# Memory attention in ten small steps, the compressed branch in nine, and groups begun one unit earlier

## The chip, the cores and the metric

The kernel runs on one core of one Trainium2 chip. The metric is the time of one execution in device microseconds (us); of several runs the median counts. Engines are named as in the profile: PE (TensorE), DVE (VectorE), ACT (ScalarE), POOL (GpSimd), SP (the queue that issues the weight loads).

## What is computed

A transformer block with three mixers and a feed-forward part, followed by two layers of a second kind, on a sequence of 512 tokens of 1024 features, all in fp32. Three pieces matter here. The memory attention has four heads over 256 memory tokens:

```python
s = jnp.einsum('bshd,bmhd->bhsm', qh, k).astype(jnp.float32) * MEM_SCALE
p = jax.nn.softmax(s, axis=-1).astype(v.dtype)
return jnp.einsum('bhsm,bmhd->bshd', p, v).reshape(B, S, MEM_W)
```

The sparse attention has 16 heads in four groups, and three branches with a sigmoid gate each; the compressed branch attends to 31 averaged blocks of keys:

```python
s = jnp.einsum('bsghd,bngd->bghsn', q, kc) * NSA_SCALE
p = masked_softmax(s, end[None, :] <= t[:, None])
o = jnp.einsum('bghsn,bngd->bsghd', p.astype(vc.dtype), vc)
...
y_nsa = (gb[..., 0:1] * o_cmp + gb[..., 1:2] * o_slc + gb[..., 2:3] * o_win).reshape(B, S, NSA_Q)
```

The three mixers are then merged, `y` being the sum that the last projection completes:

```python
y = (gm[:, :, 0] * (y_nsa @ w_proj_nsa[l]) + gm[:, :, 1] * (y_ml @ w_proj_ml[l])
     + gm[:, :, 2] * (y_mem @ w_proj_mem[l]))
```

## The kernel before

All weights stream through SBUF in units of four or eight blocks of 128 x 128. To keep fp32 precision every operand is split into a high half (a cast to fp32r on ACT) and a low half (the difference, on DVE): for weights `whi` (L96) and `wlo` (L97), for activations the helper `split` (L241, L242). One product is then three matmuls (high-high, low-high, high-low, helper `mm` at L224), and one block of a unit is a step of three matmuls. SP loads a unit five units ahead, ACT and DVE split it three units ahead, between the other work of their queues.

The order of work is that in which the program issues instructions; each engine runs its own part of it in order. `mix_items` (L1619) writes the list of units. A `Mix` lays a generator between the steps of its units: it gets so many pulls, spread evenly over the steps, and with `drain` the generator is run to its end there. `Side` lets a generator go on beside the units that follow. `em.defer(n, f)` issues f some n steps later.

`mem_pair` (L1279) is a generator for two memory heads: `score` issues the score matmuls (ps_ms, 128 x 512), DVE's maximum and its negation (mmx), ACT's exponentials (mp), and DVE's reciprocal and scaling; `turn` transposes on PE (ps_mt) and splits (mpth, mptl); `values` multiplies with the values (ps_mo) and splits. Pair 0 lies between the four units that give the keys and values of the compressed branch, whose results leave a bank of ps_z by two copies on DVE (cz, L1224 and L1225) and two on ACT (cmpAk, L1226 and L1227), and beside `ml_final`, a normalisation on DVE (mfy, mfr). Pair 2 lies between gate units (ACT's sg, L1537) and projections.

`nsa_group` (L1366) treats one of four groups of sparse attention in 38 pulls. Pulls 0 to 31 each begin one of 32 scores (ps_sc; 4 heads, 2 branches, 4 blocks of 128 to 512 columns); a pull also carries the earlier scores on: maximum (smx) one pull later, exponential (pf) two, reciprocal and scaling three, transposition on PE (ps_tr) four, and its split (pth on ACT, ptl on DVE, L1484) five pulls later:

```python
stages = ((score, 0), (turn, 4), (recip, 3), (rowmax, 1), (scale, 3), (evict, 5), (low, 5), (expo, 2))
```

The compressed branch is tied to some pulls by `extra`. It shares the three banks of scores (psc) and the two banks of transposes (ptr) with the rest. Before each group come its key unit, two query units (whose split moves halves by DMA, L1347 and L1348) and its values' unit, which ends in a transposition (ps_tt) and DVE's split of the values (vs). The group's pulls are spread over fill units (merge gates and projections, 48 steps), and what is left is drained in the next group's first two units; that of the last group runs beside `p1`, the last eight projections. In `proj_unit` (L1541) a projection's result is multiplied with its gate (yt) and added to y (L1556), both on DVE; the last pass then splits y.

Of the kernel before, what the change touches and what calls it, by code (L numbers as in the profile page):

```python
# [204 lines left out]
class Model:  # L205
# [1073 lines left out]
    def mem_pair(self, h0):  # L1279
# [3 lines left out]
        pr, pt_ = {}, {}  # L1283

        def score(h, hf):
            qh, ql = self.qm[h]
            ps = self.psc.tile([P, 2, 256], F32, tag="sc", name="ps_ms")
            for t in range(2):
                xs = slice((2 * hf + t) * P, (2 * hf + t + 1) * P)
                self.mm3(ps[:, t, :], qh[:, xs], ql[:, xs], self.mk_h[:, h, :], self.mk_l[:, h, :], True, True)  # L1290
            mx = t2.tile([P, 2], F32, tag="mmx", name="mmx", bufs=3)
            nc.vector.tensor_reduce(out=mx, in_=ps, axis=AX.X, op=OP.max)
            nc.vector.tensor_scalar(out=mx, in0=mx, scalar1=-sc, scalar2=None, op0=OP.mult)
            p = t2.tile([P, 2, 256], F32, tag="mp", name="mp", bufs=3)
            sm = t2.tile([P, 2], F32, tag="msm", name="msm", bufs=3)
            for t in range(2):
                nc.scalar.activation(out=p[:, t, :], in_=ps[:, t, :], func=AF.Exp, scale=sc, bias=mx[:, t:t + 1],
                                     accum_out=sm[:, t:t + 1])
            nc.vector.reciprocal(mx, sm)
# [3 lines left out]
            pr[h, hf] = p  # L1303

        def turn(h, hf):
            p = pr.pop((h, hf))
# [10 lines left out]
        def values(h):  # L1317
# [5 lines left out]
            self.split(self.bh[h], self.bl[h], po)  # L1323

        h1 = h0 + 1
        for step in (((score, h0, 0),), ((score, h0, 1),), ((score, h1, 0),), ((turn, h0, 0),),
                     ((turn, h0, 1), (score, h1, 1)), (), ((values, h0), (turn, h1, 0)), ((turn, h1, 1),), (),
                     ((values, h1),)):
            for f, *args in step:
                f(*args)  # L1330
            yield

# [33 lines left out]
    def nsa_group(self, g):  # L1366
# [7 lines left out]
        def c_score():  # L1374
            kc = self.kc[:, g].rearrange("p c n -> p (c n)")
            cs = t3.tile([P, S], F32, tag="cpf", name="cs")
            for i in range(0, 4, 2):
                pc = self.psc.tile([P, 2, 4, 64], F32, tag="sc", name="ps_c")
                for t in range(2):
                    for j in range(4):  # L1380
                        self.mm(pc[:, t, j, :], qs[j][:, (i + t) * P:(i + t + 1) * P], kc, True, True)
                c = cs.rearrange("p (i j n) -> p i j n", i=4, j=4)[:, i:i + 2]
                nc.vector.tensor_tensor(out=c, in0=pc[:, :, :, 0:32],
                                        in1=self.maskc[:, i:i + 2].unsqueeze(2).to_broadcast([P, 2, 4, 32]), op=OP.add)
                nc.vector.tensor_tensor(out=c, in0=pc[:, :, :, 32:64], in1=c, op=OP.add)
            mx = t3.tile([P, 16], F32, tag="cmx", name="cmx")
# [3 lines left out]
            cst["p"], cst["m"] = cs, mx  # L1390
# [4 lines left out]
        def c_norm():  # L1395
            ce, mx = cst["p"], cst["m"]
            sm = t3.tile([P, 16], F32, tag="csm", name="csm")
# [5 lines left out]
            nc.vector.tensor_scalar(out=sm[:, 0:4], in0=sm[:, 0:4], scalar1=self.rowv, scalar2=None, op0=OP.mult)  # L1403
            nc.vector.tensor_tensor(out=f3(ce), in0=f3(ce), in1=sm.unsqueeze(2).to_broadcast([P, 16, 32]), op=OP.mult)
# [7 lines left out]
        def c_evict():  # L1412
            self.split(pch, pcl, cst["t"])
# [3 lines left out]
        extra = {2: c_score, 3: c_exp, 4: c_norm, 7: c_turn, 8: c_evict}  # L1417
# [123 lines left out]
    def proj_unit(self, name, idx, m, hl, first, last=False):  # L1541
# [7 lines left out]
        def done(ps):  # L1549
# [69 lines left out]
    def mix_items(self):  # L1619
# [114 lines left out]
        items += qkv[0]  # L1734
# [211 lines left out]
```

## Time and profile before

| | before |
|---|---|
| median of 3 runs | 2894.15 us (2893.62 to 2895.26) |
| the profiled execution | 2895.78 us, span of its instructions 2893.8 us |
| busy: PE, DVE, ACT, POOL | 2832.3, 1593.5, 1132.5, 29.6 us |
| mean granted clock of PE | 0.989 |

The span runs from the first to the last instruction of the profiled execution, and all starts below count from its begin. Busy time of PE overlaps: matmuls are pipelined, each is listed longer than the distance to the next. PEclk is the share of full speed that was granted.

### The profile page before, as it was taken

The page shows a single profiled execution, that of the slowest core. Times are in us where ns is not written, and L with a number is a line of the kernel's source. Part 1 is how long each engine was busy: PE and PEld are TensorE (multiplying, and loading weights), DVE is VectorE, ACT ScalarE, POOL GpSimd, SP SyncE. Part 2 cuts the span into 40 slices and gives each one's busy share as a digit, 9 for nine tenths or more (in the row PEclk, how much of TensorE's full clock was granted, in tenths as well). Part 3 has the DMA queues.
Part 4 walks back from the last instruction along what each step waited for, and adds up shares of the span by engine and source line. Part 5 has one row for each costly group of instructions (what it writes and reads, how often), then busy time and mean ns, then how long its engine had stood idle before and what let it go on. Part 6 is the DMA issues. An engine that isn't in the chain of part 4 may idle for free.

```text
span 2893.8 us, 33730 instructions
## 1 busy us (share of the span) xinstructions
PE 2832.3 (98%) x13103; PEld 2317.8 (80%) x13103; DVE 1593.5 (55%) x2504; ACT 1132.5 (39%) x1993; POOL 29.6 (1%) x111
## 2 busy tenths in 40 slices
PE   8999999999999999999999999999999999999998
PEld 6778787787788888788888888888888887788887
DVE  7765577778664344643447434454344588654443
ACT  6453355555342222422335322333223466532223
POOL 0000000000000000000000000000000000000000
PEclk9999999999999999999999999999999999999999
DMA  5222321221322323323222223232232311132322
GB/s 178 73 71 88 91 66 59 66 70 34 131 91 87 107 93 97 103 89 108 93 81 88 96 87 110 80 108 96 88 109 81 102 52 37 66 110 81 109 82 78
DMA packets 83951, 255.86 MB, mean 88 GB/s; under 512 B 9648, under 2 KB 11312, under 8 KB 83792
## 3 DMA queue, kind: packets, MB, share of 16 engines
q1 hardware_dynamic: 78528, 243.03, 26.5%
q0 software_dynamic: 3968, 8.59, 1.2%
q8 instruction: 102, 1.67, 0.2%
q10 hardware_dynamic: 1296, 2.10, 0.2%
q14 instruction: 57, 0.47, 0.1%
HBM read 246.86 MB, written 2.10 MB: 86 GB/s over the span
## 4 chain that ended last, share of the span: by engine, by line
PE 90%; DVE 6%; ACT 2%; issue 1%; DMA 0%; SPq 0%; DVEq 0%; ACTq 0%
PE ps_d L224 21%; PE ps_g L224 21%; PE ps_u L224 21%; PE ps_z L224 9%; PE ps_t L224 4%; PE ps_pj L224 2%; PE ps_c L224 2%; PE ps_pv L224 2%; PE ps_b L224 2%; PE ps_a L224 2%; PE ps_o L224 2%; PE ps_sc L224 1%; PE ps_tr L1467 1%; DVE wlo L97 1%; ACT whi L96 1%
## 5 line engine op out<-in xcount | busy, mean ns | idle before, releaser
L97 DVE TENSOR_TENSOR wlo<-raw,whi 128x1024 fp32r<-128x1024 f32 (+3 forms) x519 | 561.0, 1084 | 571.0 <-ACT whi L96 568.9
L96 ACT CAST whi<-raw 128x1024 fp32r<-128x1024 f32 (+3 forms) x519 | 483.8, 936 | 585.1 <-PE ps_d L224 259.9
L224 PE MATMUL ps_g<-xh,whi 128*128 128x512 f32 x880 | 345.5, 393 | 4.6 <-ACT xh L447 4.6
L224 PE MATMUL ps_d<-hh,whi 128*128 128x512 f32 x880 | 345.9, 393 | 0.0
L224 PE MATMUL ps_d<-hh,wlo 128*128 128x512 f32 x880 | 345.0, 392 | 0.0
L224 PE MATMUL ps_g<-xl,whi 128*128 128x512 f32 x880 | 343.8, 391 | 1.0 <-DVE xl L449 1.0
L224 PE MATMUL ps_d<-hl,whi 128*128 128x512 f32 x880 | 344.7, 392 | 0.0
L224 PE MATMUL ps_u<-xh,whi 128*128 128x512 f32 x880 | 343.9, 391 | 0.0
L224 PE MATMUL ps_g<-xh,wlo 128*128 128x512 f32 x880 | 343.4, 390 | 0.0
L224 PE MATMUL ps_u<-xl,whi 128*128 128x512 f32 x880 | 342.9, 390 | 0.0
L224 PE MATMUL ps_u<-xh,wlo 128*128 128x512 f32 x880 | 342.8, 390 | 0.0
L377 DVE TENSOR_TENSOR fu<-ps_u,R 128x512 f32<-128x512 f32 x110 | 75.9, 690 | 272.5 <-PE ps_u L224 272.5
L241 ACT CAST hh<-fh 128x512 fp32r<-128x512 f32 x110 | 68.4, 621 | 360.7 <-DVE fh L379 360.7
L224 PEld LDWEIGHTS ps_g<-xh,whi 128*128 128x128 f32 x880 | 166.0, 189 | 40.4 <-ACT xh L447 5.2
L224 PEld LDWEIGHTS ps_g<-xl,whi 128*128 128x128 f32 x880 | 165.9, 189 | 36.8 <-DVE xl L449 2.0
L224 PEld LDWEIGHTS ps_d<-hh,wlo 128*128 128x128 f32 x880 | 165.0, 188 | 37.7
L224 PEld LDWEIGHTS ps_d<-hl,whi 128*128 128x128 f32 x880 | 165.2, 188 | 37.2
L224 PEld LDWEIGHTS ps_d<-hh,whi 128*128 128x128 f32 x880 | 165.1, 188 | 37.0
L224 PEld LDWEIGHTS ps_g<-xh,wlo 128*128 128x128 f32 x880 | 165.9, 189 | 34.7
L224 PEld LDWEIGHTS ps_u<-xh,whi 128*128 128x128 f32 x880 | 165.6, 188 | 35.0 <-issue 0.5
L224 PEld LDWEIGHTS ps_u<-xl,whi 128*128 128x128 f32 x880 | 165.6, 188 | 34.8 <-issue 0.5
L224 PEld LDWEIGHTS ps_u<-xh,wlo 128*128 128x128 f32 x880 | 165.6, 188 | 34.6
(471 smaller groups left out, 4393.1 us busy)
## 6 DMA issues: line engine op xcount, KB each, us to landing
raw<-in_f2in_dram SPq DMA_DIRECT2D x176, 512.0 KB, 3.3
raw<-in_wz_dram SPq DMA_DIRECT2D x64, 512.0 KB, 3.3
raw<-in_f2dn_dram SPq DMA_DIRECT2D x64, 384.0 KB, 3.1
raw<-in_f1in_dram SPq DMA_DIRECT2D x44, 512.0 KB, 3.3
raw<-in_f2dn_dram SPq DMA_DIRECT2D x64, 320.0 KB, 2.9
raw<-in_pw_dram SPq DMA_DIRECT2D x24, 512.0 KB, 3.4
raw<-in_f1dn_dram SPq DMA_DIRECT2D x16, 384.0 KB, 3.1
raw<-in_f1dn_dram SPq DMA_DIRECT2D x16, 320.0 KB, 2.9
```

The costliest lines, as they stand in the source:

```text
L96: self.nc.scalar.copy(hi[:, 0:n], r)
L97: fn = lambda: self.nc.vector.tensor_tensor(out=lo[:, 0:n], in0=r, in1=hi[:, 0:n].bitcast(F32), op=OP.subtract)
L224: self.nc.tensor.matmul(out, lhsT, rhs, start=start, stop=stop)
L241: nc.scalar.copy(hi, src)
L377: nc.vector.tensor_tensor(out=u, in0=ps, in1=self.R, op=OP.mult)
L1467: nc.tensor.transpose(ps[:, s * P:(s + 1) * P], p[:, s * P:(s + 1) * P], self.ident)
```

## The change

`mem_pair` is cut into smaller steps. Exponentials, normalisation and the low halves of the two splits become functions of their own, each issued one pull or more after what it needs. In `nsa_group` the compressed branch takes pulls 2 to 10 instead of 2 to 8, with its score in two halves. In `mix_items` a group's generator begins in its values' unit with 3 pulls, and the fill carries 28 pulls (31 for the last group) instead of 34; the drain in the next two units then has 7 left instead of 4. In `proj_unit` the addition to y goes from DVE to POOL in the last pass, and the split of y comes 5 steps later instead of 3.

```diff
@@ mem_pair
-        def score(h, hf):
+        def score(n):
...
             nc.vector.tensor_reduce(out=mx, in_=ps, axis=AX.X, op=OP.max)
             nc.vector.tensor_scalar(out=mx, in0=mx, scalar1=-sc, scalar2=None, op0=OP.mult)
+            st[n] = ps, mx
+
+        def expo(n):
...
+        def scale(n):
+            p, mx, sm = st[n]
             nc.vector.reciprocal(mx, sm)
...
-        def turn(h, hf):
+        def turn(n):
...
-            self.split(pt_[h][0][:, :, xs], pt_[h][1][:, :, xs], pt)
+            nc.scalar.copy(pt_[h][0][:, :, xs], pt)
+            st[n] = pt
+
+        def low(n):
...
+            nc.vector.tensor_tensor(out=lo, in0=st.pop(n), in1=hi.bitcast(F32), op=OP.subtract)
...
-            self.split(self.bh[h], self.bl[h], po)
+            nc.scalar.copy(self.bh[h], po)
...
-        for step in (((score, h0, 0),), ((score, h0, 1),), ((score, h1, 0),), ((turn, h0, 0),),
-                     ((turn, h0, 1), (score, h1, 1)), (), ((values, h0), (turn, h1, 0)), ((turn, h1, 1),), (),
-                     ((values, h1),)):
+        for step in (((score, 0),), ((expo, 0), (score, 1)), ((expo, 1), (scale, 0), (score, 2)),
+                     ((expo, 2), (scale, 1), (turn, 0)), ((scale, 2), (low, 0), (turn, 1), (score, 3)),
+                     ((expo, 3), (low, 1)), ((values, 0), (turn, 2), (scale, 3)), ((halves, 0), (low, 2), (turn, 3)),
+                     ((low, 3),), ((values, 1),)):
@@ nsa_group
-        extra = {2: c_score, 3: c_exp, 4: c_norm, 7: c_turn, 8: c_evict}
+        extra = {2: lambda: c_score(0), 3: lambda: c_score(2), 4: c_max, 5: c_exp, 6: c_sum, 7: c_scale, 8: c_turn,
+                 9: c_evict, 10: c_low}
@@ proj_unit
-                nc.vector.tensor_tensor(out=self.y[m], in0=self.y[m], in1=y, op=OP.add)
+                (nc.gpsimd if last else nc.vector).tensor_tensor(out=self.y[m], in0=self.y[m], in1=y, op=OP.add)
             if last:
-                self.em.defer(3, lambda: self.split(*self.xslot(m), self.y[m], 0.5))
+                self.em.defer(5, lambda: self.split(*self.xslot(m), self.y[m], 0.5))
@@ mix_items
-        items += qkv[0]
+        gens = [lazy(lambda g=g: self.nsa_group(g)) for g in range(4)]
+        head = lambda g: qkv[g][2:3] + [Mix(qkv[g][3:4], gens[g], 3)]
+        items += qkv[0][0:2] + head(0)
...
-            gen = lazy(lambda g=g: self.nsa_group(g))
-            items.append(Mix(fill[g], gen, 34))
+            items.append(Mix(fill[g], gens[g], 28 if g < 3 else 31))
             if g < 3:
-                items += [Mix(qkv[g + 1][0:2], gen, 7, True)] + qkv[g + 1][2:]
+                items += [Mix(qkv[g + 1][0:2], gens[g], 7, True)] + head(g + 1)
             else:
-                items.append(Side(gen))
+                items.append(Side(gens[g]))
```

The order of instructions at three places. First ACT in the first memory pair, before (mp are the exponentials, cmpAk the copies that empty a bank of ps_z, whi a cast of weights):

```order
L96 CAST whi<-raw 128x1024
L1297 ACT_TABLE_LOAD
L1297 ACTIVATE mp,msm<-ps_ms,mmx 128x256 x6
L96 CAST whi<-raw 128x1024
L1226 COPY cmpAk<-ps_z 64x256
L1227 COPY cmpAk<-ps_z 64x256
L241 CAST mpth<-ps_mt 128x2x256 x2
L1297 ACTIVATE mp,msm<-ps_ms,mmx 128x256 x2
```

and now:

```order
L96 CAST whi<-raw 128x1024
L1303 ACT_TABLE_LOAD
L1303 ACTIVATE mp,msm<-ps_ms,mmx 128x256 x4
L96 CAST whi<-raw 128x1024
L1226 COPY cmpAk<-ps_z 64x256
L1227 COPY cmpAk<-ps_z 64x256
L1303 ACTIVATE mp,msm<-ps_ms,mmx 128x256 x2
L1326 CAST mpth<-ps_mt 128x2x256 x2
```

The exponentials of the third score (two instructions) moved behind the copies cmpAk, and behind them come the casts mpth.

Second, DVE at the start of group 0, before (vs is the split of the values, cs the scores of the compressed branch, cmx their maximum, smx, src and pf belong to the group's own scores):

```order
L97 TENSOR_TENSOR wlo<-raw,whi 128x512
L242 TENSOR_TENSOR vs<-ps_tt,vs 128x8x64
L1435 TENSOR_REDUCE smx<-ps_sc 128x1 x2
L1383 TENSOR_TENSOR cs<-ps_c,maskc 128x256
L1385 TENSOR_TENSOR cs<-ps_c,cs 128x256
L1383 TENSOR_TENSOR cs<-ps_c,maskc 128x256
L1385 TENSOR_TENSOR cs<-ps_c,cs 128x256
L1387 TENSOR_REDUCE cmx<-cs 128x16
L1388 TENSOR_TENSOR cs<-cs,cmx 128x512
L1450 RECIPROCAL src<-ssm 128x1
L1435 TENSOR_REDUCE smx<-ps_sc 128x1
L1458 TENSOR_SCALAR pf<-pf,src,gsig 128x128
```

and now:

```order
L1469 TENSOR_REDUCE smx<-ps_sc 128x1 x2
L1408 TENSOR_TENSOR cs<-ps_c,maskc 128x256
L1410 TENSOR_TENSOR cs<-ps_c,cs 128x256
L97 TENSOR_TENSOR wlo<-raw,whi 128x512
L1484 RECIPROCAL src<-ssm 128x1
L1469 TENSOR_REDUCE smx<-ps_sc 128x1
L1492 TENSOR_SCALAR pf<-pf,src,gsig 128x128
L1408 TENSOR_TENSOR cs<-ps_c,maskc 128x256
L1410 TENSOR_TENSOR cs<-ps_c,cs 128x256
L242 TENSOR_TENSOR vs<-ps_tt,vs 128x8x64
L1484 RECIPROCAL src<-ssm 128x1
L1469 TENSOR_REDUCE smx<-ps_sc 128x1
```

The split vs now stands behind both halves of the compressed scores and the first normalisation (pf of 128 columns); it was ahead of all of them.

Third, PE where the compressed branch is transposed (ps_ct), before (ps_tr are the transposes of the group's own scores, ps_sc its scores, ps_pv its value products):

```order
L224 MATMUL ps_sc<-ks,qs 128x512 x2
L224 LDWEIGHTS identb
L224 MATMUL ps_sc<-mask_q,identb 128x128
L1467 MATMUL ps_tr<-ident,pf 128x128 x4
L1409 MATMUL ps_ct<-ident,cs 128x128 x4
L224 MATMUL ps_pv<-pth,vs 128x256
L224 MATMUL ps_pv<-ptl,vs 128x256
```

and now:

```order
L224 MATMUL ps_sc<-ks,qs 128x128 x2
L224 LDWEIGHTS identb
L224 MATMUL ps_sc<-mask_q,identb 128x128
L1501 MATMUL ps_tr<-ident,pf 128x128
L1439 MATMUL ps_ct<-ident,cs 128x128 x4
L224 MATMUL ps_pj<-bh,whi 128x512
L224 MATMUL ps_pj<-bl,whi 128x512
```

ps_ct follows the transposition of the fifth score (128 columns) where it followed that of the fourth (512 columns), and a step of a projection follows it.

## Rows read from the trace of the kernel before

**Rows 1.** The page's first part: busy us of the engine.

```profile
PE 2832.3 (98%) x13103; PEld 2317.8 (80%) x13103; DVE 1593.5 (55%) x2504; ACT 1132.5 (39%) x1993; POOL 29.6 (1%) x111
```

**Rows 2.** The waits of PE: who for whom: us in total, times, longest.

```profile
PE ps_tr L1467 <- DVE ptl L1484: 9.8, 7, 2.1
...
PE ps_z L224 <- ACT cmpAk L1227: 4.4, 1, 4.4
...
PE ps_pj L224 <- DVE yt L1552: 1.3, 2, 0.7
...
PE ps_pj L224 <- ACT sg L1537: 0.7, 1, 0.7
```

**Rows 3.** Windows: length, busy us of each engine, PEclk, DMA share, GB/s.

```profile
206.67:213.49 6.82, 5.57 (x13) 4.41 (x14) 4.85 (x11) 3.98 (x10) 1.05 (x2) 0.50 0.32 97
455.84:459.25 3.41, 3.23 (x9) 2.68 (x10) 2.55 (x9) 1.20 (x6) 0.00 (x0) 0.50 0.25 77
```

**Rows 4.** Timeline, first memory pair: start, us, engine, instruction, [idle before, releaser].

```profile
197.40 0.17 DVE L1299 RECIPROCAL mmx<-msm 128x2 f32<-128x2 f32 x1 [2.45 <-ACT mp L1297]
...
201.38 0.70 PE L1313 MATMUL ps_mt<-ident,mp 128*128 128x128 f32 x4 [0.57 <-DVE mp L1301]
...
205.07 1.23 DVE L97 TENSOR_TENSOR wlo<-raw,whi 128x1024 fp32r<-128x1024 f32 x1
...
207.12 0.37 ACT L1226 COPY cmpAk<-ps_z 64x256 f32<-64x256 f32 x1 [2.08 <-DVE cz L1225]
...
207.92 0.79 PE L224 MATMUL ps_z<-xh,whi 128*128 128x512 f32 x1 [4.42 <-ACT cmpAk L1227]
...
213.57 0.39 PE L224 MATMUL ps_z<-xl,whi 128*128 128x512 f32 x1
213.79 0.40 PE L224 MATMUL ps_z<-xh,wlo 128*128 128x512 f32 x1
```

**Rows 5.** Timeline, start of group 0 (its first step at 343.9).

```profile
342.56 0.39 PE L224 MATMUL ps_t<-xh,wlo 128*128 128x512 f32 x1
...
345.14 0.60 PE L941 MATMUL ps_tt<-ident,tok 128*128 128x128 f32 x4
...
347.83 1.97 PE L224 MATMUL ps_c<-kc,qs 128*128 128x64 f32 x16
...
355.76 0.23 PE L224 MATMUL ps_sc<-mask_q,identb 128*128 128x128 bf16 x1
358.07 0.55 PE L1467 MATMUL ps_tr<-ident,pf 128*128 128x128 f32 x3 [2.08 <-DVE ptl L1484]
...
359.84 0.62 PE L224 MATMUL ps_sc<-ks,qs 128*128 128x512 f32 x2
...
346.40 0.69 DVE L242 TENSOR_TENSOR vs<-ps_tt,vs 128x512 fp32r<-128x512 f32 x1 [1.58 <-ACT vs L241]
...
350.76 0.69 DVE L1387 TENSOR_REDUCE cmx<-cs 128x16 f32<-128x512 f32 x1
...
352.09 0.15 DVE L1450 RECIPROCAL src<-ssm 128x1 f32<-128x1 f32 x1
...
352.87 0.15 DVE L1450 RECIPROCAL src<-ssm 128x1 f32<-128x1 f32 x1
...
360.46 0.69 DVE L97 TENSOR_TENSOR wlo<-raw,whi 128x512 fp32r<-128x512 f32 x1
```

**Rows 6.** Timeline, last projection: DVE, then PE.

```profile
733.33 0.68 DVE L1552 SCALAR_TENSOR_TENSOR yt<-z,ps_pj 128x512 f32<-128x512 f32 x1
734.04 0.69 DVE L1556 TENSOR_TENSOR y<-y,yt 128x512 f32<-128x512 f32 x1
...
736.39 0.68 DVE L1552 SCALAR_TENSOR_TENSOR yt<-z,ps_pj 128x512 f32<-128x512 f32 x1
...
734.16 0.47 PE L224 MATMUL ps_pj<-bh,whi 128*128 128x512 f32 x1 [0.71 <-DVE yt L1552]
```

**Rows 7.** Groups by line, POOL: count, busy us, mean ns.

```profile
L1611 POOL TENSOR_SCALAR_AFFINE_SELECT maskc<-maskc 128x128 f32<-128x128 f32 x1 | 0.3, 310 | 0.1
```

More of the change, by code (lines that the diff above doesn't have):

```diff
@@ L1282, in mem_pair @@
         sc = 128.0 ** -0.5
-        pr, pt_ = {}, {}
-        def score(h, hf):
+        st, pt_ = {}, {}
+        who = [(h0, 0), (h0, 1), (h0 + 1, 0), (h0 + 1, 1)]
+        def score(n):
+            h, hf = who[n]
             qh, ql = self.qm[h]
@@ L1298, in score @@
                                      accum_out=sm[:, t:t + 1])
+            st[n] = p, mx, sm
+        def scale(n):
+            p, mx, sm = st[n]
             nc.vector.reciprocal(mx, sm)
@@ L1302, in score @@
                                         op0=OP.mult)
-            pr[h, hf] = p
-        def turn(h, hf):
-            p = pr.pop((h, hf))
+            st[n] = p
+        def turn(n):
+            p = st[n]
+            h, hf = who[n]
             if hf == 0:
@@ L1314, in turn, with values @@
             xs = slice(hf * 256, (hf + 1) * 256)
-            self.split(pt_[h][0][:, :, xs], pt_[h][1][:, :, xs], pt)
-        def values(h):
+            nc.scalar.copy(pt_[h][0][:, :, xs], pt)
+            st[n] = pt
+        def low(n):
+            h, hf = who[n]
+            xs = slice(hf * 256, (hf + 1) * 256)
+            hi, lo = (t[:, :, xs] for t in pt_[h])
+            nc.vector.tensor_tensor(out=lo, in0=st.pop(n), in1=hi.bitcast(F32), op=OP.subtract)
+        def values(i):
+            h = h0 + i
             pth, ptl = pt_.pop(h)
@@ L1322, in values, with halves @@
                 self.mm3(po, self.mv_h[:, c, hs], self.mv_l[:, c, hs], pth[:, c, :], ptl[:, c, :], c == 0, c == 1)
-            self.split(self.bh[h], self.bl[h], po)
-        h1 = h0 + 1
-        for step in (((score, h0, 0),), ((score, h0, 1),), ((score, h1, 0),), ((turn, h0, 0),),
-                     ((turn, h0, 1), (score, h1, 1)), (), ((values, h0), (turn, h1, 0)), ((turn, h1, 1),), (),
-                     ((values, h1),)):
-            for f, *args in step:
-                f(*args)
+            nc.scalar.copy(self.bh[h], po)
+            st["o", i] = po
+        def halves(i):
+            h = h0 + i
+            nc.vector.tensor_tensor(out=self.bl[h], in0=st.pop(("o", i)), in1=self.bh[h].bitcast(F32), op=OP.subtract)
+        for step in (((score, 0),), ((expo, 0), (score, 1)), ((expo, 1), (scale, 0), (score, 2)),
+                     ((expo, 2), (scale, 1), (turn, 0)), ((scale, 2), (low, 0), (turn, 1), (score, 3)),
+                     ((expo, 3), (low, 1)), ((values, 0), (turn, 2), (scale, 3)), ((halves, 0), (low, 2), (turn, 3)),
+                     ((low, 3),), ((values, 1),)):
+            for f, n in step:
+                f(n)
             yield
+        halves(1)
     def q_evict(self, ps, j):
@@ L1371, in nsa_group, with c_score, c_max @@
         cst = {}
-        def c_score():
+        def c_score(i):
             kc = self.kc[:, g].rearrange("p c n -> p (c n)")
[L1376 to L1386, printed above, removed]
+            if i == 0:
+                cst["p"] = t3.tile([P, S], F32, tag="cpf", name="cs")
+            pc = self.psc.tile([P, 2, 4, 64], F32, tag="sc", name="ps_c")
+            for t in range(2):
+                for j in range(4):
+                    self.mm(pc[:, t, j, :], qs[j][:, (i + t) * P:(i + t + 1) * P], kc, True, True)
+            c = cst["p"].rearrange("p (i j n) -> p i j n", i=4, j=4)[:, i:i + 2]
+            nc.vector.tensor_tensor(out=c, in0=pc[:, :, :, 0:32],
+                                    in1=self.maskc[:, i:i + 2].unsqueeze(2).to_broadcast([P, 2, 4, 32]), op=OP.add)
+            nc.vector.tensor_tensor(out=c, in0=pc[:, :, :, 32:64], in1=c, op=OP.add)
+        def c_max():
+            cs = cst["p"]
+            mx = cst["m"] = t3.tile([P, 16], F32, tag="cmx", name="cmx")
             nc.vector.tensor_reduce(out=mx, in_=f3(cs), axis=AX.X, op=OP.max)
@@ L1412, in c_evict, with c_low @@
         def c_evict():
-            self.split(pch, pcl, cst["t"])
+            nc.scalar.copy(pch, cst["t"])
+        def c_low():
+            nc.vector.tensor_tensor(out=pcl, in0=cst["t"], in1=pch.bitcast(F32), op=OP.subtract)
         pch = t3.tile([P, S], F32R, tag="pch", name="pch")
         pcl = t3.tile([P, S], F32R, tag="pcl", name="pcl")
-        extra = {2: c_score, 3: c_exp, 4: c_norm, 7: c_turn, 8: c_evict}
+        extra = {2: lambda: c_score(0), 3: lambda: c_score(2), 4: c_max, 5: c_exp, 6: c_sum, 7: c_scale, 8: c_turn,
+                 9: c_evict, 10: c_low}
         steps = [(j, b, i) for j in range(4) for b in range(2) for i in range(4)]
```

8 lines of the change are left out of this document (5 added, 3 removed).

## The prediction

> **What bounds the kernel now.** The page's first part comes first: TensorE (PE) is busy for 2832.3 of 2893.8 us [rows 1]. The change issues the same matmuls, so what it can win or lose is time in which PE waits, and time in which PE runs at the lower clock. The next view is therefore the waits of PE [rows 2]. Of its sums, only these belong to code that the change touches: 9.8 us in seven waits of ps_tr for the DVE subtraction ptl (groups of sparse attention), 4.4 us in one wait of ps_z for the ACT copy cmpAk and 0.7 us for ACT's sg (the two pairs of memory heads), 1.3 us in two waits for DVE's yt (the last projection). The four group starts hold 2.08 us each of the 9.8; the other three waits share the rest, about 0.5 each.
>
> A wait as listed understates the loss, because PE's last matmul is still draining when the wait begins. I count from start to start: the wait listed as 2.08 us spans 355.76 to 358.07 [rows 5], 2.25 us more than the 0.06 that a transpose needs behind a score. With two smaller gaps before it (0.4 and 0.2 by the same count) a group start loses 2.85 us.
>
> The third view is the granted clock by windows [rows 3]. PE stands at 0.50, that is 1.2 instead of 2.4 GHz, for 6.82 us from 206.67 in the first memory pair, and for 3.41 us from 455.84, at the start of group 1; another such stretch, from 653.8 at the start of group 3, reads alike. The same wait in groups 0 and 2 has none. In the first stretch 13 matmuls take 207.92 to 213.57 [rows 4], 5.65 us; at the 0.22 to 0.23 us of full clock (213.57 to 213.79) they need 2.95, so 2.7 us are lost. Of 3.4 us about half, 1.6, is lost, twice.
>
> **First memory pair.** The timeline [rows 4] shows a convoy. DVE's reciprocal at 197.40 waited 2.45 us for ACT's exponentials, which wait in turn for the maxima that DVE puts out behind it. ACT's queue runs in order, so the two copies cmpAk stand behind the exponentials of three scores and a weight cast; the first also waits 2.08 us for DVE's cz. PE needs the bank that they empty, and starts at 207.92 instead of 203.3. Loss: 4.6 there, 0.75 at 201.38 (the second transposition), 2.7 by the clock, together 8.0 us.
>
> In the changed order the maxima no longer stand behind the normalisation, and the third exponential stands behind cmpAk on ACT. I add the same instructions at the spacing they have now. The reciprocal still starts at 197.40; with scales, maximum and negation (0.2 + 0.55 + 0.7 + 0.2) DVE is at 199.05, waits to 199.3 for the weight cast that ACT begins after the second exponential, and needs 2.05 us (205.07 to 207.12) for wlo and both cz: 201.3. The copies cmpAk end at 202.1; PE wants their bank at about 204.5, so **the 4.6 us go**. What is late next is the second transposition: behind cz, DVE still has one mfr (0.7), a reciprocal (0.2) and the scale, so it starts at 202.5 where PE arrives at 200.7: 1.8 instead of 0.75. The first value product then waits for a subtraction that now stands behind wlo and two cz: by the same adding it ends at 209.0, and PE is there at 208.1, about 0.9. New loss 2.7, **gain 5.3**. Whether the lower clock follows waits of 1.8 and 0.9 no row shows: the bounds are none and a stretch of 1.6, and I take none, as a wait of 2.25 had one in only two of four.
>
> **Second pair.** PE waits for sg, which stands on ACT behind exponentials that waited for DVE. In the new order those exponentials come a step later, behind it. Gain 0.7 as listed [rows 2], 0.9 with the draining of PE; nothing else of this pair makes PE wait.
>
> **Group starts.** The group now begins in its values' unit: three of its scores stand between the matmuls of that unit, so the transposition ps_tt, on which DVE's value split waits, moves back. From the last matmul of the unit (342.79 is its end) I add three scores (128, 256 and 384 columns; one of 512 is listed with 0.62 [rows 5], so with its mask some 0.2 + 0.35 + 0.5), three steps of three matmuls (2.1), one score of 512 (0.6), the two halves of ps_c (together 1.8; the 16 matmuls are listed with 1.97), and 0.35 for the changes of shape: ps_tt starts at 348.7 instead of 345.14. The split on DVE follows 1.26 later, as now (345.14 to 346.40), at 349.95. Everything of DVE's queue behind the split waits with it.
>
> From there DVE has no gap in either order. Before, it runs from c_max at 350.76 to the end of the third ptl at 360.46, 9.70 us. In the new order, up to the ptl of score 3, it does the same set, less one reciprocal, maximum and scale (352.09 to 352.87, 0.78), plus the value split (0.6), plus one more such trio (about 1.0) and the ptl of 512 columns (0.6): 11.1 us, ending at 361.1. The compressed branch's transposition ps_ct waits for just that ptl, since the pool of transposes has two banks. PE's work from ps_tt to ps_ct is eight steps of three matmuls (0.69 each), five scores (1.9), transposes and ps_tt (1.3), four short value products (0.5) and changes of shape (0.5), 9.7 us: it arrives at 358.4. **Loss 2.75 where 2.85 stood**: the wait moves from the third transposition to ps_ct and keeps its size. Group 3 has 31 pulls instead of 28 over the same fill, so PE arrives about 0.6 earlier and waits longer by that. Sum over four groups: +0.2. I leave the clock's stretches as they are, two of four (3.2 us); bounds none and four, so -3.2 and +3.2.
>
> **Middle and end of a group.** With 48 steps' fill given to 28 pulls instead of 34, DVE has more PE time per pull. The three late waits (0.6 each by starts) sat where pulls were densest: I take them as gone, **-1.8**, bounds 0 and -1.8. The seven pulls left for the next two units, instead of four, lie where PE does not wait now; I cost them at nothing, covered by 48 matmuls of those units.
>
> **Last projection.** A DVE period there is 733.33 to 736.39, 3.06 us, against 12 matmuls of PE at 0.23, 2.8 us [rows 6]. The addition to y (0.69 long, 0.61 with the overlap of the next instruction) goes to POOL; DVE is left with 2.45, and PE's wait at 734.16 (0.85 by starts) goes: **-0.8**, bounds 0 and -1.6 (both waits). POOL has never done such an addition in this trace; the nearest row is its selection over 128 columns, 310 ns [rows 7], so 1.2 us for 512, taken as an estimate. There is one yt buffer, so the next product on DVE waits for POOL; there is room up to about 2.1 us.
> The Trainium skill speaks against this part: the GPSIMD Engine Reference, section 3.1, has the addition of two inputs at 2.6 cycles an element, twice VectorE's time, and section 1 says that POOL shares its SBUF interface with VectorE and contends with instructions of two SBUF inputs. By its measured 4497 ns for 2048 elements the addition would take an estimated 1.1 us, inside the room; no row here shows either rule.
>
> **The sum.** -5.3 - 0.9 + 0.2 - 1.8 - 0.8 = -8.6; I round to -8, since each term assumes that the small waits do not come back elsewhere. The profiled execution took 2895.8 us, the median is 2894.15; from the median the forecast is **2886.2 us**, from the profiled one 2887.8. With 3.2 us of clock either way and the small bounds, its own range is 2882 to 2890.
>
> **Rivals.**
> (B) *The group starts hide completely.* If the split of the values comes out earlier than I add, ps_ct finds its bank free, and the stretches of low clock go too: another 4 x 2.75 + 3.2, down to 2872; half of it, 2879. For it: DVE has the whole values' unit to begin in. Against it: DVE works without a gap from the split on. Chance 0.13.
> (C) *Each group start becomes what the first memory pair is now*, a wait of 4.6 us followed by 2.7 us at the lower clock, 7.3 instead of 2.75 + 0.8. The place is ps_ct behind the ptl of score 3; it needs DVE's chain to end 1.9 us later, for example because the split is held on ACT. +3.75 x 4 on -8: 2901, slower. It decides from 2 us more a group. For it: the split heads DVE's queue, in front of the whole chain. Against it: ACT is free around 349. Chance 0.08.
> (D) *POOL's addition holds DVE.* If DVE's instructions stand still while POOL adds (1.2 us), a period is 2.45 + 1.2, 0.9 over PE's, in the three last units and 0.4 in the four with half-size weights: +4.3 and no gain of 0.8, 2891. Section 1 of the GPSIMD Engine Reference in the Trainium skill, as told above, describes this case. For it: wlo has two SBUF inputs. Against it: no row. Chance 0.12.
> (E) *The convoy in the first pair stays.* If DVE still waits for ACT there, with the copies as late as now, 5.3 are missing: 2891.5. For it: 1.8 us of wait remain even in my sum. Against it: cmpAk is past the exponentials on ACT. Chance 0.14.
> The forecast has 0.53.
>
> **How the numbers follow.** Two executions differ by about 1.6 us here; 0.2%, 5.8 us, is about what a measurement can tell from no change. Faster by more than that (under 2888.4): most of the forecast (0.45) and B, 0.58. Within it: the rest of the forecast, D and E, 0.34. Slower: C, 0.08. The range leaves out C and the far half of B: 2878 to 2893.5.
>
> **What would show it.** Right: PE's wait for cmpAk is gone and the window from 187 has no half-clock stretch; ps_ct, not ps_tr, waits for ptl, about 2.3 us four times; POOL shows eight additions between 0.9 and 1.5 us, with yt not waiting. Wrong: a wait over 3 us in either place, a ps_ct that does not wait, yt waiting for POOL, or more half-clock stretches than two among the group starts.

## The result, and the profile after

The changed kernel takes 2912.14 us (2909.85 to 2914.48) where the one before takes 2894.7 beside it: a ratio of 1.0059, interval 1.0048 to 1.0071. It is **slower by 17.4 us**, where 8 us less were forecast. The span grew from 2893.8 to 2911.1 us.

PE's busy time grew by 4.0 us against [rows 1], and its mean granted clock hardly changed (0.989 before, 0.990 now). The page's first part after:

```profile
PE 2836.3 (97%) x13103; PEld 2318.0 (80%) x13103; DVE 1586.6 (55%) x2496; ACT 1132.8 (39%) x1993; POOL 42.2 (1%) x119
```

So most of the loss, 13.3 of 17.3 us, is new idle time of PE. The waits of PE after (who for whom: us in total, times, longest), which answer to [rows 2]:

```profile
PE ps_tr L1501 <- DVE ptl L1518: 15.6, 14, 2.3
PE ps_ct L1439 <- DVE ptl L1518: 8.0, 4, 2.7
...
PE ps_tr L1501 <- DVE src L1484: 3.2, 3, 1.1
...
PE ps_mt L1324 <- DVE mp L1311: 1.7, 1, 1.7
...
PE ps_pj L224 <- DVE yt L1586: 1.0, 2, 0.6
...
PE ps_sc L224 <- DMA qs<-qt: 0.8, 3, 0.3
...
PE ps_mo L224 <- DVE mptl L1333: 0.6, 1, 0.6
```

The waits for cmpAk and sg are gone, as forecast, with two small ones in their place (ps_mt, ps_mo), and ps_ct waits four times, as forecast. But ps_tr, whose 9.8 us were to vanish, waits for 15.6 us behind ptl and for 3.2 behind src. New too are three small waits of scores for the query halves that are moved by DMA (qs). The windows, which answer to [rows 3] (the first memory pair whole, and the end of group 0):

```profile
190.00:224.00 34.00, 31.59 (x153) 25.27 (x152) 25.33 (x50) 18.11 (x40) 3.41 (x7) 1.00 0.24 79
425.30:428.71 3.41, 3.41 (x10) 2.63 (x9) 0.00 (x0) 0.00 (x0) 0.00 (x0) 0.50 0.00 0
```

The first memory pair now runs at the full 2.4 GHz. Three stretches at 1.2 GHz, all 3.41 us long, have come at 425.3, 531.1 and 636.9; a fourth stands at the start of group 3, at 671.1.

Where the loss lies is read from one mark in both traces, the first matmul of each group's values' unit:

| first matmul of | before | after | gained so far | lost in this period |
|---|---|---|---|---|
| values' unit, group 0 | 337.35 | 330.95 | 6.4 | -6.4 |
| group 1 | 435.31 | 435.88 | -0.6 | +7.0 |
| group 2 | 534.59 | 541.71 | -7.1 | +6.55 |
| group 3 | 632.56 | 647.52 | -15.0 | +7.84 |
| first gate of the second part (ps_g) | 792.86 | 810.11 | -17.25 | +2.3 |

The memory part gains what was forecast, and each of the first three groups gives back about 7 us. Counted from start to start, group 0 now loses 2.0 at ps_ct with 0.6 just before it, 0.6 at 358.7, 1.55 at 394.2, 1.25 at 405.5 and 2.49 at 420.5. Behind the last of these stands the low clock, which costs 1.7 more. The places repeat every 105.8 us in groups 1 and 2. Group 3, with its 31 pulls, loses 2.85 at ps_ct, 1.5 at 677.4 and 0.6 at 692.1.

The largest is at the **end** of a group, in the two units that now carry seven left pulls. Timeline after, group 0:

```profile
417.63 1.05 ACT L96 CAST whi<-raw 128x1024 fp32r<-128x1024 f32 x1 [2.00 <-PE ps_z L224]
...
418.59 0.57 ACT L241 CAST ks<-ps_z 64x512 fp32r<-64x512 f32 x1
...
418.72 1.22 DVE L97 TENSOR_TENSOR wlo<-raw,whi 128x1024 fp32r<-128x1024 f32 x1 [2.23 <-ACT whi L96]
...
419.86 0.68 DVE L242 TENSOR_TENSOR ks<-ps_z,ks 64x512 fp32r<-64x512 f32 x1
...
420.57 0.58 ACT L241 CAST ks<-ps_z 64x512 fp32r<-64x512 f32 x1 [1.41 <-DVE ks L242]
...
421.17 0.75 ACT L1514 CAST pth<-ps_tr 128x256 fp32r<-128x256 f32 x2
421.18 0.69 DVE L242 TENSOR_TENSOR ks<-ps_z,ks 64x512 fp32r<-64x512 f32 x1 [0.65 <-ACT ks L241]
421.91 0.16 DVE L1484 RECIPROCAL src<-ssm 128x1 f32<-128x1 f32 x1
422.11 0.55 DVE L1492 TENSOR_SCALAR pf<-pf,src,gsig 128x512 f32<-128x512 f32 x1
...
422.68 0.89 DVE L1518 TENSOR_TENSOR ptl<-ps_tr,pth 128x256 fp32r<-128x256 f32 x2
```

And the same place before, where the last transposition of the group (score 31) waits for nothing:

```profile
418.13 0.55 DVE L1458 TENSOR_SCALAR pf<-pf,src,gsig 128x512 f32<-128x512 f32 x1
...
419.65 0.60 PE L1467 MATMUL ps_tr<-ident,pf 128*128 128x128 f32 x4
```

The key unit of the next group ends in `k_evict`, the split of the keys (ks: two casts on ACT, two subtractions on DVE). With four left pulls, the transposition of score 31 is the second of them and comes ahead of that split. With seven it is the fifth, comes after the twelfth of 16 steps, and falls behind it. DVE then has wlo, two ks and the last score's scaling in front of ptl, and ACT's casts pth stand behind a ks cast that waited 1.41 us. PE waits 2.3 us for ptl, at 423.25.

The two waits in the **middle** stand behind other work of DVE's queue. Timeline after, the first of them (whole lines of DVE and PE):

```profile
391.60 1.23 DVE L97 TENSOR_TENSOR wlo<-raw,whi 128x1024 fp32r<-128x1024 f32 x1 [0.16 <-ACT whi L96]
...
392.75 0.68 DVE L1586 SCALAR_TENSOR_TENSOR yt<-z,ps_pj 128x512 f32<-128x512 f32 x1
...
393.46 0.69 DVE L1590 TENSOR_TENSOR y<-y,yt 128x512 f32<-128x512 f32 x1
...
395.05 0.68 DVE L1518 TENSOR_TENSOR ptl<-ps_tr,pth 128x512 fp32r<-128x512 f32 x1
...
395.79 0.44 PE L1501 MATMUL ps_tr<-ident,pf 128*128 128x128 f32 x2 [1.38 <-DVE ptl L1518]
```

and the second:

```profile
402.77 1.05 ACT L96 CAST whi<-raw 128x1024 fp32r<-128x1024 f32 x1 [2.42 <-PE ps_z L224]
...
403.86 1.22 DVE L97 TENSOR_TENSOR wlo<-raw,whi 128x1024 fp32r<-128x1024 f32 x1 [3.38 <-ACT whi L96]
...
405.98 0.68 DVE L1518 TENSOR_TENSOR ptl<-ps_tr,pth 128x512 fp32r<-128x512 f32 x1
...
406.81 0.41 PE L1501 MATMUL ps_tr<-ident,pf 128*128 128x128 f32 x2 [1.09 <-DVE src L1484]
```

At 392.75 the end of a projection (yt and the addition to y) comes just ahead of a score's reciprocal, scaling and ptl. At 402.77 the cast of the next weights waits 2.42 us until PE is done with the buffer it overwrites, and ACT's queue and then DVE's are held up behind it.

### The profile page after: what moved, and what is told of

Same layout as the page of the kernel before. It is cut to its first block, busy times and chain, and to the rows that moved or that the text cites. A ratio compares the mean times of both kernels' runs of the same rounds, so it can differ in the third digit from the quotient of the medians.

```text
span 2911.1 us, 33741 instructions
## 1 busy us (share of the span) xinstructions
PE 2836.3 (97%) x13103; PEld 2318.0 (80%) x13103; DVE 1586.6 (55%) x2496; ACT 1132.8 (39%) x1993; POOL 42.2 (1%) x119
## 3 DMA queue, kind: packets, MB, share of 16 engines
q8 instruction: 102, 1.67, 0.2%
## 4 chain that ended last, share of the span: by engine, by line
PE 88%; DVE 6%; ACT 3%; issue 2%; DMA 0%; POOL 0%; SPq 0%; DVEq 0%; ACTq 0%; POOLq 0%
PE ps_d L224 21%; PE ps_g L224 21%; PE ps_u L224 21%; PE ps_z L224 7%; PE ps_t L224 4%; PE ps_pj L224 2%; PE ps_c L224 2%; PE ps_b L224 2%; PE ps_a L224 2%; PE ps_o L224 2%; PE ps_pv L224 1%; PE ps_sc L224 1%; DVE wlo L97 1%; PE ps_tr L1501 1%; ACT whi L96 1%
## 5 line engine op out<-in xcount | busy, mean ns | idle before, releaser
L224 PE MATMUL ps_u<-xh,whi 128*128 128x512 f32 x880 | 343.9, 391 | 0.0
```

The source lines that it names most:

```text
L224: self.nc.tensor.matmul(out, lhsT, rhs, start=start, stop=stop)
```

## The experiments

From this came the theories. T: the loss comes from where the pulls now fall (28 over the fill and 7 left), against the unit boundaries and the key split. R1: it comes from the nine steps of the compressed branch. R2: it comes from beginning a group in its values' unit. For single places: W, the weight cast that waits for PE's buffer holds ACT and DVE; P, the projection's end stands ahead of ptl. Rival D of the prediction (POOL holds DVE) was tried by itself. Ratios are against the kernel before on the same chip.

**The parts alone.** The first run is the kernel before with the new `mem_pair` and nothing else.

> Only the memory pairs in small steps; sparse attention, its pacing and the last projection as before. All theories agree that this part helps: the start of group 0 is reached 5.8 us earlier in the changed kernel's trace than before, and a little of that is the start of the program. Expected: 2889 us (2888 to 2890), 5.5 us under the kernel before, no half-clock stretch at the first pair. If it is not below 2892, the gain seen in the trace of the changed kernel came from elsewhere.

2890.02 us, ratio 0.998 (0.997 to 0.9989): 5.7 us gained, about the 6.2 forecast for both pairs. The memory part of the change is right by itself.

The second gives all groups 31 pulls, so that four are left as before:

```diff
-            items.append(Mix(fill[g], gens[g], 28 if g < 3 else 31))
+            items.append(Mix(fill[g], gens[g], 31))
```

> The change, but with 31 pulls in the fill of every group instead of 28, so that 4 pulls instead of 7 are left for the next group's first two units, as before the change. Theory T (the loss is at the end of a group, where seven pulls meet the split of the next keys on ACT and DVE: 2.5 us of wait and 1.7 us of low clock in each of three groups): 2912 - 3 x 4.2 = 2899, give or take 3 for other waits that move. Rival R1 (the nine steps of the compressed branch are at fault, by ps_ct one pull later): 2910 or more. Rival R2 (the early beginning delays the values' split and with it all of the group): 2910 or more.

2902.79, ratio 1.0027 (1.0017 to 1.0036). The end wait of 2.49 is gone, with its low clock, and 9.4 of the 12.6 us that T expected are gained. A group still loses 0.58, 2.83 (ps_ct), 1.53, 0.61 and 1.09, and the late wait of before (0.7) is back in the first three: waits at the start and in the middle remain.

The third takes `mix_items` from before (no early beginning, 34 pulls, four left) and keeps the rest of the change, the fourth keeps `mix_items` and takes the old five steps:

```diff
-        gens = [lazy(lambda g=g: self.nsa_group(g)) for g in range(4)]
-        head = lambda g: qkv[g][2:3] + [Mix(qkv[g][3:4], gens[g], 3)]
-        items += qkv[0][0:2] + head(0)
+        items += qkv[0]
...
-            items.append(Mix(fill[g], gens[g], 28 if g < 3 else 31))
+            items.append(Mix(fill[g], gen, 34))
```

> The change without the early beginning and without the new numbers of pulls: groups begin behind their values' unit and get 34 pulls in the fill, 4 are left; memory pairs, nine steps and the addition on POOL are kept. T and R2: both losses belong to what is undone here, so 2894.7 - 5.5 (memory) - 0.7 (projection) = 2888.5, plus what the nine steps do at a group start, 0 to 1 us each: 2887 to 2892. R1: about 2905, since the nine steps are still there.

2891.19, ratio 0.9985 (0.9976 to 0.9995). With the old beginning and the old pulls the whole loss goes; each group has 1.25 and 2.30 at its start, and the first three have the late wait of before (0.7).

```diff
-        extra = {2: lambda: c_score(0), 3: lambda: c_score(2), 4: c_max, 5: c_exp, 6: c_sum, 7: c_scale, 8: c_turn,
-                 9: c_evict, 10: c_low}
+        extra = {2: c_score, 3: c_exp, 4: c_norm, 7: c_turn, 8: c_evict}
```

> The change with the compressed branch in its old five steps (pulls 2, 3, 4, 7, 8); the early beginning and 28 pulls are kept. T and R2: the loss stays, 2908 to 2916. R1: it goes, 2888 to 2893. The start of a group should show one wait of about 2 us, at a transposition of the group's own scores or at ps_ct.

2910.87, ratio 1.006 (1.0043 to 1.0077). The loss stays without the nine steps: R1 falls. What the early beginning costs by itself no run separates: the second run keeps it, together with its 31 pulls, and is 11.6 us above the third.

**The end of a group.** The next two leave seven pulls, but move score 31's transposition ahead of the key split, or straighten the split itself (both casts, then both subtractions):

```diff
-                items += [Mix(qkv[g + 1][0:2], gens[g], 7, True)] + head(g + 1)
+                items += [Mix(qkv[g + 1][0:1], gens[g], 5), Mix(qkv[g + 1][1:2], gens[g], 2, True)] + head(g + 1)
```

> The change, but of the seven pulls that are left behind the fill, five lie in the next group's key unit and two in the query unit behind it; in the change they are spread over both, and the transposition of the last score (the fifth of the seven pulls) comes after the split of the new keys. Theory T (the wait of 2.3 us and the low clock behind it come because the casts pth of the last scores stand on ACT behind that split): they go, 3 x 4.2 = 12.6 off 2912, 2899.5 (2897 to 2903). Rival L (seven pulls are simply too much for DVE in these units): the wait moves into the key unit and stays, 2907 or more.

> The change, with the split of the new keys issued as two casts on ACT and then two subtractions on DVE, instead of cast, subtraction, cast, subtraction; in the changed kernel ACT's second cast waited 1.4 us for DVE's first subtraction, and pth stood behind it. Theory T: the wait of 2.3 us at the last transposition shrinks by about 1 us in three groups and the low clock may go: 2912 - 3 x (1 to 2.7) = 2904 to 2909. Rival L: nothing changes, 2911 to 2913.

The first takes 2905.99, ratio 1.0037 (1.0023 to 1.0052), the second 2910.06, 1.0051 (1.0036 to 1.0066). Timeline of the first at the end of group 0:

```profile
415.19 0.44 PE L1501 MATMUL ps_tr<-ident,pf 128*128 128x128 f32 x2 [1.12 <-DVE ptl L1518]
```

and of the second:

```profile
420.04 0.76 ACT L1517 CAST pth<-ps_tr 128x256 fp32r<-128x256 f32 x2
...
421.74 0.55 DVE L1495 TENSOR_SCALAR pf<-pf,src,gsig 128x512 f32<-128x512 f32 x1
...
422.89 0.52 PE L1504 MATMUL ps_tr<-ident,pf 128*128 128x128 f32 x3 [1.71 <-DVE ptl L1521]
```

Ahead of the split, PE still waits 1.1 us, but without low clock behind it, and 6.2 of the 12.6 us that T expected are gained: the result lies between T and L. DVE has no gap there from 409.16 until ptl ends at 415.14, so what is left is work that five pulls in one unit bring together. Straightened, pth is cast 1.1 us earlier (420.04, not 421.17), yet ptl still stands behind wlo, both ks and the scaling of score 31, and 0.6 of the wait goes; low clock follows it in one group of three.

**The weights' casts.** Splitting the weights two units ahead instead of three, from the sparse attention on, frees the buffer sooner. It was tried on the change until the end of the last projections, in the memory-only kernel likewise, and on the change with a return to three before the last projections:

```diff
+        items.append(lambda: setattr(self.em, "SPLIT_AHEAD", 2))
...
+        items.append(lambda: setattr(self.em, "SPLIT_AHEAD", 3))
```

> The change, with weights split two units ahead instead of three as long as sparse attention and its projections run. In the changed kernel ACT waits at the cast whi for PE to finish the unit whose buffer it overwrites (2.4 us at 402.8), with pth and the exponentials behind it, and DVE waits for the cast. Theory W (this is what the two new waits of 1.4 and 1.1 us in the middle of each group are, and a part of the one at its end): they go, 3 x (1.5 + 1.2) = 8, and 1 to 4 us more at each end: 2895 to 2904. Rival P (the middle waits come from DVE's work alone: wlo, product, addition and ptl of 512 columns fall together in the new pacing): less than 3 us change, 2909 or more.

> The memory pairs in small steps alone, with weights split two units ahead during sparse attention and its projections. Theory W: the group starts of the old order wait for DVE alone, with no whi in the chain but its wlo of 1.1 us, which now falls elsewhere: up to 1.1 us less at each of four starts and the three late waits of 0.6 gone, 2890 - 0 to 6 = 2884 to 2890. Rival P: as the memory pairs alone, 2889 to 2891, or later where a weight now comes too late, 2892 or more.

> As the run with weights split two units ahead, but with three units ahead again from the first projection of the last pass on, so that the 10.3 us wait and the 10.2 us of low clock behind the last projection, which that run made itself, are gone. Theory W (whi on ACT waits for PE, and pth and wlo behind it): the wait of 1.2 us in the middle is gone, the one at the end of a group is 1.1 instead of 2.5 and has no low clock behind it: 2912 - 3 x (1.2 + 1.4 + 1.7) = 2899, with new small waits up to 2903. Rival P (DVE's work alone): 2908 or more.

The first two tell little: 2913.04, ratio 1.0062 (1.0045 to 1.0078), and 2899.75, 1.0016 (1.0007 to 1.0026). Both have a wait of their own where they return to three, 10.3 and 7.5 us, with 10.24 and 6.83 us at 1.2 GHz that begin inside it. The third has none: 2901.45, 1.0024 (1.0015 to 1.0033), 10.7 us less than the change. ACT's waits of whi for PE, 28.1 us in 17 between 340 and 640 in the change, are not among those of this run. The wait of 1.25 is gone and the end wait falls from 2.49 to 1.12, without low clock behind it. The wait of 1.55 stays (1.56), and the one at 358.7 grows from 0.6 to 1.57. So W is right for the second middle wait and a part of the end; it does not explain the first middle wait.

**The pace alone, and POOL alone.** The memory-only kernel with 31 pulls for 34 has neither the nine steps nor the early beginning, but seven pulls left:

```diff
-            items.append(Mix(fill[g], gen, 34))
+            items.append(Mix(fill[g], gen, 31))
```

> The memory pairs in small steps alone, groups begun behind their values' unit as before, but with 31 pulls instead of 34 in each fill, so that seven are left for the next two units. This has the seven late pulls without the early beginning and without the nine steps. Theory T: at the end of each of three groups the wait of about 2.5 us comes, with or without 1.7 us of low clock: 2890 + 3 x 2.5 to 4.2 = 2897 to 2903. Rival R2 (the early beginning is the cause): 2888 to 2892.

2925.12, ratio 1.0097 (1.008 to 1.0113), 35 us above the memory-only kernel. Its waits of PE:

```profile
PE ps_tr L1492 <- DVE ptl L1509: 22.3, 22, 2.3
PE ps_tr L1492 <- DVE src L1475: 8.4, 7, 1.3
```

The end wait is there (2.51), with 1.2 GHz behind it for 6.83, 3.41 and 6.83 us, and before it one wait of 1.8 and seven of 0.5 to 1.5 in group 0. Fewer pulls in the fill are enough to make this loss; the early beginning is not needed for it, so R2 falls as its sole cause. T named the direction, but the size is far above its expectation; why the middle waits are larger here than in the change is open.

The other run gives all 24 additions to y to POOL (`nc.gpsimd` for `nc.vector` in `proj_unit`), again on the memory-only kernel:

> The memory pairs in small steps alone, with every addition to y on POOL (24 instead of none). In the changed kernel the addition took 1.67 us there, and DVE's wlo beside it 1.9 to 2.2 us instead of 1.2. Theory D (POOL's addition holds DVE's instructions that read two tensors from SBUF): DVE saves 0.6 and loses up to 1 us for each addition; group starts wait longer or as long, the last projection gains 0.3: 2889 to 2896. Rival (POOL's work is free for DVE): the three late waits of 0.6 and 0.9 in the last projection go, 2886 to 2888.

2893.8, ratio 0.9995 (0.9985 to 1.0004), 3.8 us more than the memory-only kernel. DVE's weight subtractions between 340 and 740, by line (count, busy us, mean ns), with the additions on POOL:

```profile
L97 DVE TENSOR_TENSOR wlo<-raw,whi 128x1024 fp32r<-128x1024 f32 x29 | 38.0, 1310 | 30.3 <-ACT whi L96 30.1
```

and in the memory-only kernel:

```profile
L97 DVE TENSOR_TENSOR wlo<-raw,whi 128x1024 fp32r<-128x1024 f32 x29 | 35.5, 1224 | 29.9 <-ACT whi L96 29.6
```

The addition on POOL stretches them: rival D's mechanism exists. It also stretches DVE's scaling pf where that begins under an addition, as 7 of 32 do with 512 columns. With the additions on POOL, and then in the memory-only kernel:

```profile
L1483 DVE TENSOR_SCALAR pf<-pf,src,gsig 128x512 f32<-128x512 f32 x32 | 23.4, 731 | 0.1
...
L1483 DVE TENSOR_SCALAR pf<-pf,src,gsig 128x512 f32<-128x512 f32 x32 | 17.3, 540 | 0.1
```

**The first middle wait.** P was tried by issuing the projection's end two steps later:

```diff
-            self.em.defer(2, lambda: done(ps))
+            self.em.defer(2 if last or first else 4, lambda: done(ps))
```

> The change, with product and addition of a projection issued four steps behind it instead of two in the middle passes, so that at the wait of 1.55 us (at 394.2 in the changed kernel, a transposition that waits for ptl of 512 columns) they stand behind that ptl on DVE and not ahead of it. Theory P (this wait is DVE's work that falls together: value split, wlo, product, addition, maximum, scaling, ptl): the wait goes in three groups, 3 x 1.3 to 1.55 = 4 to 5, with other small waits that come or go: 2905 to 2910. If the wait stays, something other than DVE's queue holds ptl there.

Timeline at the place of that wait:

```profile
394.07 0.69 DVE L1518 TENSOR_TENSOR ptl<-ps_tr,pth 128x512 fp32r<-128x512 f32 x1
...
394.67 0.68 DVE L1586 SCALAR_TENSOR_TENSOR yt<-z,ps_pj 128x512 f32<-128x512 f32 x1
...
394.81 0.44 PE L1501 MATMUL ps_tr<-ident,pf 128*128 128x128 f32 x2
```

ptl is now ahead of yt and PE does not wait; this holds in all three groups, and P is right for this wait. The time does not show it: 2912.38, ratio 1.0058 (1.0043 to 1.0073). The mean granted clock of its four runs is 0.988 against 0.990 of the change. 0.002 of 2900 us, 5.8 us, is about what the wait was worth in three groups, so the lower clock would account for it; why the clock was lower is open. The profiled executions show the gain where both have the same low clock, 13.65 us: from the first matmul of group 0's values' unit to the first of the unit behind the last projection (ps_o), this run takes 421.9 us and the change 427.5 (the wait of 0.6 at 358.7 went as well).

**A version that beats both.** The memory-only kernel keeps the old pace and the old beginning, and spreads the compressed branch over pulls with a gap behind the score halves and behind the sum. The first value product moves one score later with it.

```diff
+        extra = {2: lambda: c_score(0), 4: lambda: c_score(2), 5: c_max, 6: c_exp, 7: c_sum, 9: c_scale, 10: c_turn,
+                 11: c_evict, 12: c_low}
...
-            if b == 1 and hf == 0:
+            if b == 1 and hf == 1:
```

> The memory pairs in small steps, groups begun and paced as before, and the compressed branch spread over pulls 2 to 12: score halves at 2 and 4, maximum 5, exponential 6, sum 7, scaling 9, transposition 10, its split 11 and 12; its value product moves to the last value product of each head, so that it is in time. If a group start is bound by DVE's work between the values' split and the transposition, spreading that work gives PE its time: the 2.85 us of each start fall to 0.5 to 1.5, and the stretches of low clock behind them go: 2890 - 4 x 1.5 to 2.3 - 0 to 3 = 2878 to 2884. If the waits only move to other transpositions, as in the nine steps: 2888 to 2894.

> The run with the compressed branch spread over pulls 2 to 12, with weights split two units ahead in sparse attention as well. If whi on ACT and wlo behind it are a part of the waits that are left at its group starts (0.6, 1.1 and 1.3 us), these shrink: 2881 to 2886. If they are DVE's work alone, 2886 to 2888; if weights come too late somewhere, above 2888.

2886.68, ratio 0.9968 (0.9956 to 0.998), the lowest of all, though above the 2878 to 2884 that were expected. A group start loses 0.63, 1.08 and 1.30 in place of 2.25 and its smaller gaps: 3.0 in sum, not less than the 2.85 before. Its waits of PE, and the window of the sparse attention:

```profile
PE ps_tr L1501 <- DVE ptl L1518: 7.0, 11, 0.9
...
PE ps_ct L1439 <- DVE ptl L1518: 4.6, 4, 1.1
```

```profile
330.00:740.00 410.00, 396.70 (x2245) 322.02 (x2244) 307.61 (x725) 216.33 (x529) 10.23 (x20) 1.00 0.21 65
```

No wait is above 1.1 us here, and PE stands at the full clock throughout. In the traces, that is where the gain lies: from one values' unit to the next the memory-only kernel takes 98.1, 99.3 and 98.0 us and this one 98.0 each time, and the 99.3 are those of group 1, at whose start the memory-only kernel has 3.41 us at 1.2 GHz (its other such stretch is in group 3, where this kernel gains 1.2). The waits were broken up, not hidden. With the weights two units ahead it is not better (2888.47, 0.9978, 0.9969 to 0.9988): the first three group starts lose 1.61 and 1.30, so what is left there is not the weights' queue.

## Why the prediction was wrong

**The step that failed** is "Middle and end of a group". It took the three late waits of 0.6 "as gone, -1.8", because DVE gets more PE time per pull, and cost the seven left pulls "at nothing, covered by 48 matmuls". Measured, a group's middle lost 3.4 (0.6, 1.55 and 1.25), where 0.6 stood before and nothing was forecast, and its end 4.2 (2.49 and 1.7 by the clock) instead of nothing. That is 7 us more in each of three groups, the 21 us of the table. Two errors are in that step:

- The cover was counted as an amount. DVE is busy for 55% of the span, and 48 matmuls are 11 us; but what decides is what stands just ahead of one ptl in DVE's order. The order of instructions was read at three places, and not at this one, where score 31's transposition passes the key split and DVE's wlo stands behind a weight cast that waits for PE (2.00 us). Each of the two was moved by itself, and each took a part of the end's wait (2.49 to 1.3 and to 1.12) and the low clock with it.
- Fewer pulls do give DVE more time each, but they also move every score against the weight splits and projection ends, which did not move. The late wait of before (0.7 by starts) was not where pulls were densest, since they are spread evenly over the fill. It stood where a weight split, the split of a head's result (a) and the work of several scores met, with no gap on DVE from 409.95 to the end of ptl at 414.60. Timeline before:

```profile
409.95 1.23 DVE L97 TENSOR_TENSOR wlo<-raw,whi 128x1024 fp32r<-128x1024 f32 x1 [0.30 <-ACT whi L96]
...
412.34 0.68 DVE L242 TENSOR_TENSOR a<-yv,a 64x512 fp32r<-64x512 f32 x1
...
414.65 0.44 PE L1467 MATMUL ps_tr<-ident,pf 128*128 128x128 f32 x2 [0.49 <-DVE ptl L1484]
```

No rival named this place. C, the slower one, had a mechanism of this kind, a longer wait followed by low clock, at the group start; it happened at the group end. None of the forecast's signs of being wrong came either: no wait at the places named was over 3 us, ps_ct waited, yt did not wait for POOL, and one group start had a stretch at 1.2 GHz. They all looked at places whose price was nearly right, and none at a term that was put at nothing.

Point by point, the rest:

- **First memory pair**: gain of 5.3 forecast and 0.9 for the second pair; the trace after has, counted by starts, waits of 1.85 (forecast 1.8) and 0.8 (0.9), no low clock, and 5.9 gained by the mark in the table (6.4 less 0.5 that already differ ahead of the pair). The memory-only run gives 5.7. Right, and rival E is out.
- **Group starts**: the split was to begin at 349.95, which is 343.55 after the 6.4 gained, and begins at 343.31; the ptl of 512 columns was to end at 354.7 by the same shift, and ends at 354.25. The loss was to be 2.75 and is 2.0 at ps_ct in groups 0 to 2 (2.6 with the wait just before it); in group 3 it was to be 3.35 and is 2.85. Right in kind, and somewhat too dear; rival B did not come.
- **Low clock at the starts**: left at two of four, 3.2 us; only group 3 has one at its start now, while three came to the ends.
- **Last projection**: -0.8 forecast; the wait went from 0.85 to 0.55, and one of 0.2 came a unit earlier. The addition takes 1.58 us on POOL on average, not 1.2, and it does hold DVE. Groups by line after, on POOL:

```profile
L1590 POOL TENSOR_TENSOR y<-y,yt 128x512 f32<-128x512 f32 x8 | 12.6, 1578 | 98.1 <-DVE yt L1586 98.1
```

The timeline of POOL in the last projections:

```profile
752.04 1.67 POOL L1590 TENSOR_TENSOR y<-y,yt 128x512 f32<-128x512 f32 x1 [1.89 <-DVE yt L1586]
755.47 1.67 POOL L1590 TENSOR_TENSOR y<-y,yt 128x512 f32<-128x512 f32 x1 [1.76 <-DVE yt L1586]
...
762.64 1.29 POOL L1590 TENSOR_TENSOR y<-y,yt 128x512 f32<-128x512 f32 x1 [2.07 <-DVE yt L1586]
```

and of DVE:

```profile
752.93 1.86 DVE L97 TENSOR_TENSOR wlo<-raw,whi 128x1024 fp32r<-128x1024 f32 x1 [0.37 <-ACT whi L96]
...
755.32 0.68 DVE L246 SCALAR_TENSOR_TENSOR xl<-y,xh 128x512 fp32r<-128x512 f32 x1
756.03 2.20 DVE L97 TENSOR_TENSOR wlo<-raw,whi 128x1024 fp32r<-128x1024 f32 x1
```

wlo takes 1.22 us alone, and 1.86 where 0.78 of it lies beside an addition, 2.20 where 1.12 does. Of the overlap some 80 to 90% is lost to DVE. It goes the other way too: six of the eight additions begin 0.16 us behind an xl of DVE and take 1.67 to 1.68, while xl keeps its 0.68; the first and the last, with no DVE instruction beside them, take 1.29. In these rows the one that begins second is stretched. The Trainium skill's rule of contention (GPSIMD Engine Reference, section 1) is borne out by them; the addition by its section 3.1, an estimated 1.1 us, is short even of the 1.29.

## What to carry to other kernels

When pulls of a generator are spread anew over fixed units, list for each engine what ends up just ahead of the instruction that PE waits for, at every unit boundary, the drained end above all: spare time on average does not tell whether one instruction in a queue that runs in order is in time. Price the units that take the leftovers like any other place, and look for work with two engines in turn (here the key split) that a late step could fall behind. A part that gains alone (here the memory pairs) should be timed alone, since a loss four times as large beside it hides it.

## What the runs showed of the hardware

- A POOL addition of 128x512 with both inputs in SBUF takes 1.28 to 1.30 us unless DVE is already at an instruction with two SBUF inputs (2 of 8 in the change, 23 of 24 with all additions on POOL), and 1.67 to 1.69 us if it is. DVE instructions that begin under the addition are stretched in turn: wlo from 1.22 to 1.86 and 2.20 us, and, with all additions on POOL, the scaling pf of 512 columns, which reads a single large tensor from SBUF, from 0.54 to between 1.33 and 1.54 us.
- Low clock behind a wait is no fixed price. A listed wait of 2.1 gave 3.41 us of 1.2 GHz in two of four group starts before; 2.3 gave it three times in three after; 1.7 with straightened casts in one of three; 2.3 with 31 pulls gave 6.83 twice and 3.41 once, and 1.3 there gave 3.41 in one group of four; 1.1 never did.
- ACT waited for a DVE instruction whose output it does not read, at two places where both only read the PSUM tile ps_z: 2.08 us for cz before [rows 4], and 1.41 us for the first ks subtraction after. So in this program the two engines' reads of one PSUM tile are put in order there; what orders them no run shows.
